# An attention output projection cut into seven half-size products in place of eight, with weight sums made by accumulating transfers

## The chip, the cores and the metric

The kernel runs on one core of a Trainium2 chip. The metric is device time in microseconds (us); lower is better. The engines are named as in the profile: PE (TensorE matmul), PEld (its weight load), DVE (VectorE), ACT (ScalarE), POOL (GpSimd), SP (SyncE, which only issues DMAs here).

## The reference

A decoder trunk of two layers on x of 512 tokens by 1024, in float32. Each layer is a token mixer and a SwiGLU FFN (1024 to 2816), each followed by a scaled residual and a layer norm:

```python
for i in range(2):
    if i == 0:
        h = multiscale_pool(x, pool_w, pool_scale)
    else:
        h = diff_attention(x, w_qkv, w_o, lam_p, subln_g, rel_table, lambda_init)
    x = layernorm(ALPHA * x + h)
    x = layernorm(ALPHA * x + (silu(x @ w_gate) * (x @ w_up)) @ w_down)
```

The causal differential attention has 8 heads with 128 value columns. Per head and token it forms `o`, divides by its root mean square, scales by `subln_g`, and puts the heads side by side to a 512x1024 matrix. Its last line is the matrix product that is changed, 512x1024 by 1024x1024:

```python
o = o * rsqrt(mean(o * o, axis=-1) + EPS)
o = o * subln_g * (1.0 - lambda_init)
return o.transpose(...).reshape(1, 512, 1024) @ w_o
```

## The kernel before

Every float32 operand is split into a high and a low part of a faster type: ACT casts x to the high part, and another engine subtracts to get the low part (`split`, lines 154 and 155). Every product is three matmuls into one PSUM bank: high by high, high by low, low by high (`mm3`, lines 180 to 182). The gate, up, down and value projections already use a seven-product scheme: both matrices are cut into two by two blocks, seven products of sums of blocks (named P1, P2, Q3, Q4, Q5, P6, P7) take the place of eight, and the sums are made beside the matmuls. The output projection does not: it multiplies whole.

All weights come from one tensor in DRAM, `wall`, as rows of 128x1024 in the order of `rows_of_wall`. `fetch` has SP load the next rows into a pool of 5 buffers (`raw`), `ready(upto)` splits them in that order into one of 6 pairs (`w96h`, `w96l`, ...). Of the rows listed in `by_dma` the low part is made by ACT (minus the raw value) and an accumulating DMA from GpSimd's queue (line 166), which adds the raw value from DRAM. All else keeps the order in which the code records it, on each engine. In the projection the rows are w96 to w103, one of each head; behind it come w104 and on, of the second FFN.

Attention goes head by head, with the work of neighbouring heads interleaved: `combine` and `split_values` prepare probabilities and values, `mix(h)` does the P·V products and the square of `o`, `root(h)` the sum of squares on PE and ACT's logarithm and exponential (lines 1372 and 1373, tile `rso`), `scaled(h)` the scaling on DVE and the split. Behind the last head's scores comes the projection. `gather(part, s, ws)` adds, for one block of 128 tokens and both column halves, the four heads of one part into two banks `wo`; part 0 is heads 0 to 3, part 1 heads 4 to 7. Between the products of part 0 stand what is left of heads 6 and 7. `residual` (line 214) adds a bank to the residual `res` on DVE, `stat`, `spread_of` and `norm` do the layer norm (POOL raises the variance to -1/2, line 230), and `turn` has PE transpose a block of the result (`pt`, line 267) for the FFN. The second FFN is called with `{0: 2, 2: 3}`: ahead of its first product it turns block 2, ahead of its third block 3.

Of the kernel before, what the change touches and what calls it, by code (L numbers as in the profile page):

```python
# [12 lines left out]
F32 = mybir.dt.float32  # L13
# [3 lines left out]
ALU = mybir.AluOpType  # L17

P = 128
# [49 lines left out]
AFFINE = {("P6", 2): (0, 1), ("P6", 3): (1, 1), ("Q3", 1): (2, 0), ("Q3", 2): (3, 0)}  # L69
GATE = ("P1", "Q5", "P6", "Q3", "P7", "P2", "Q4")  # L70
BEGUN = ("P6", "Q5", "P7", "Q3", "Q4")
PAIRS = [(0, 2), (2, 2), (4, 2), (6, 2), (8, 2), (10, 1)]


@with_exitstack
def trunk(ctx, tc, x, wall, pscale, lam_p, subln, table, lng, lnb, band, first, onehot, out):
# [6 lines left out]
    def bank(name):  # L83
        return ps.tile([P, 512], F32, tag="bank", name=name)
# [26 lines left out]
    raws = {}  # L111
    fetched = [0]
    divided = [0]
    attn = 2 + 3 * FB
    vrow = {c: attn + 2 * c for c in range(4)}
    qrow = attn + 8
# [12 lines left out]
    )  # L129
    rows_of_wall = [0, 1] + rows_of_ffn(0, 2)  # L130
    attn = len(rows_of_wall)
    rows_of_wall += order_of_rows + list(range(qrow + 2 * HEADS, qrow + 3 * HEADS))
    rows_of_wall += rows_of_ffn(1, qrow + 3 * HEADS)
    total = len(rows_of_wall)
    added = {attn + 6 + r: vrow[1] + r for r in range(2)}
    by_dma = {attn + c for c in (9, *range(12, 24))}

    def fetch(upto):
        while fetched[0] < min(upto, total):
            c = fetched[0]  # L140
            raws[c] = keep.tile([P, 1024], F32, tag="raw", name=f"raw{c}", bufs=RAWS)
            nc.sync.dma_start(out=raws[c], in_=wall[rows_of_wall[c]])
            if c in added:
                nc.gpsimd.dma_start(out=raws[c], in_=wall[added[c]], accum_op=ALU.add)
            fetched[0] += 1

    def split(dst_h, dst_l, src, scale=1.0, low=None):
        if scale != 1.0:
            nc.scalar.mul(dst_h, src, scale)
            nc.vector.scalar_tensor_tensor(  # L150
                dst_l, src, scale, dst_h.bitcast(F32), op0=ALU.mult, op1=ALU.subtract
            )
        else:
            nc.scalar.copy(dst_h, src)  # L154
            (low or nc.vector).tensor_tensor(dst_l, src, dst_h.bitcast(F32), op=ALU.subtract)  # L155

    def ready(upto, low=None):
        while divided[0] < min(upto, total):
            c = divided[0]
            fetch(c + RAWS)  # L160
            h, l = weight_pair(f"w{c}")
            raw = raws.pop(c)
            if c in by_dma:
                nc.scalar.copy(h, raw)
                nc.scalar.mul(l, raw, -1.0)
                nc.gpsimd.dma_start(
                    out=l, in_=wall[rows_of_wall[c]].bitcast(F32R), accum_op=ALU.add
                )
# [9 lines left out]
    def mm3(acc, a, b, start, stop):  # L178
        (ah, al), (bh, bl) = a, b
        nc.tensor.matmul(acc, ah, bh, start=start, stop=False)  # L180
        nc.tensor.matmul(acc, ah, bl, start=False, stop=False)  # L181
        nc.tensor.matmul(acc, al, bh, start=False, stop=stop)  # L182
# [138 lines left out]
    def turn(n, s, kept=None):  # L321
        transposed(n, s)
        turned(n, s, kept)
# [824 lines left out]
    def attention():  # L1148
        n = 2
        with tc.tile_pool(name="attn", bufs=1) as ap:  # L1150
# [52 lines left out]
            rest = xt[:, 1].rearrange("p i k t -> p (i k t)").rearrange("p (h i t) -> p h i t", h=4, i=2)  # L1203
            slots.update({16 + h: rest[:, h - 6] for h in (6, 7)})

            where = [base[0]]

# [158 lines left out]
            def root(h):  # L1366
# [6 lines left out]
                nc.scalar.activation(rs, rs, AF.Exp, scale=-0.5)  # L1373
                outs[h] = (acc, rs)

            def scaled(h):
                acc, rs = outs[h]
                nc.vector.scalar_tensor_tensor(rs, acc, gcol, rs, op0=ALU.mult, op1=ALU.mult)
                oh, ol = (slots[h if h < 6 else 16 + h][:, i, :] for i in range(2))
                split(oh, ol, rs)  # L1380
                outs[h] = (oh, ol)

            def gather(part, s, ws, between=lambda: None):
                acc = [bank(f"wo{part}_{s}_{d}") for d in range(2)]
                for js in ((0,), (1,), (2,), (3,)) if (part, s) == (0, 3) else (range(3), (3,)):
                    if js[-1] == (2 if (part, s) == (0, 3) else 3):
                        between()
                    for d in range(2):
                        for j in js:
                            mm3(  # L1390
                                acc[d],
                                tuple(t[:, s * P : (s + 1) * P] for t in outs[4 * part + j]),
                                tuple(t[:, d * 512 : (d + 1) * 512] for t in ws[j]),
                                j == 0,
                                j == 3,
                            )
                return acc

            def whole_x(t, a, b):
                nc.vector.tensor_tensor(  # L1400
# [87 lines left out]
            for h in range(HEADS):  # L1488
                if h > 0:
                    combine(h - 1, 3)  # L1490
                if h > 0:
                    split_values(h - 1)
                if h == 0:
                    scalars()
                if 1 < h <= SB + 1:
                    affine(n - 1, h - 2)
                if h == SB + 2:
                    load_gb(n)
                if h + 1 < HEADS:
                    load_bias(h + 1)  # L1500
                if h > 0:
                    accs = [bank(f"{nm}{h}") for nm in "qk"]
                    w = take(2)
                    ready(where[0] + {1: 3, last: 3}.get(h, 1))
# [5 lines left out]
                    ready(where[0] + {1: 4, last: 3}.get(h, 2))  # L1510
# [9 lines left out]
                    transposed(h - 1)  # L1520
                start_scores(h)
# [9 lines left out]
                if h == last:  # L1531
                    ready(where[0] + 4)
# [6 lines left out]
            cw = where[0]  # L1539
            combine(HEADS - 1, 3)  # L1540
            split_values(HEADS - 1)
            ws = take(4)
            between = [
                lambda: root(last - 1), lambda: transposed(last), lambda: mix(last),
                lambda: root(last),
            ]
            for s in range(SB):
                acc = gather(0, s, ws, between[s])
                if s == 0:
                    scaled(last - 1)  # L1550
                ready(cw + min(5 + s, WBUFS) if s < 3 else cw + 8)
                if s == 3:
                    scaled(last)
                for d in range(2):
                    residual(s, d, acc[d])
            ws = take(4)
            for s in range(SB):
                acc = gather(1, s, ws)
                if s == 0:
                    ready(where[0] + 1)  # L1560
                for d in range(2):
                    residual(s, d, acc[d], 1.0)
                    stat(n, s, d)
                spread_of(n, s)
                if 0 < s < 3:
                    turn(n, s - 1)
                norm(n, s)
                ready(where[0] + (min(s + 1, WBUFS - 4) if s < 3 else 4))
            base[0] = where[0]

    ffn(0, {3: 2, 5: 3})
    attention()
    ffn(1, {0: 2, 2: 3})


def buckets(rel):
# [27 lines left out]
def layout(w):  # L1604
# [37 lines left out]
    pieces.append(w["w_o"][0].reshape(HEADS, P, D))  # L1642
    ffn(1)
    return np.ascontiguousarray(np.concatenate(pieces, 0))

# [36 lines left out]
```

## Time and profile before

| | |
|---|---|
| time, median of 3 runs | 936.13 us (934.06 to 938.58) |
| profiled execution | 935.4 us, span 933.6 us |
| granted TensorE clock, mean | 0.998 |
| PE, PEld busy | 919.7, 821.5 us |
| DVE, ACT, POOL busy | 799.7, 521.0, 127.0 us |
| chain that ended last | PE 77%, DVE 12%, DMA 4%, ACT 3%, issue 2% |
| output projection | 540.5 to 590.4 us of the span |

Busy times are those of one profiled execution. A row of a timeline has start, length, engine, line, operation and tiles; a bracket behind it gives the idle time before it and what ended that. Matmuls overlap, so that the distance of two starts, not the length of one, is what a matmul takes of PE's time. A row of groups has the count, the sum, the mean of one in ns, and the idle time before.

### The profile page before, as it was taken

How to read it: one execution, taken by the hardware profiler on the slowest of the kernel's cores; microseconds unless marked ns; L12 is line 12 of the kernel's file. 1: busy time of each engine (PE TensorE's matmuls, PEld its weight loads, DVE VectorE, ACT ScalarE, POOL GpSimd, SP SyncE). 2: the span in 40 equal slices, each digit the busy share in tenths (PEclk: the TensorE clock that was granted, in tenths of full speed). 3: DMA queues.
4: the chain of work that ended last, by engine and by line, in shares of the span. 5: the costliest groups of instructions: out<-in, count | busy, mean ns of one | idle time of the engine just before them, and what ended most of it. 6: DMA issues, size and time to landing. Idle time of an engine off the chain costs nothing.

```text
span 933.6 us, 14893 instructions
## 1 busy us (share of the span) xinstructions
PE 919.7 (99%) x5662; PEld 821.5 (88%) x5662; DVE 799.7 (86%) x1186; ACT 521.0 (56%) x826; POOL 127.0 (14%) x152
## 2 busy tenths in 40 slices
PE   9999999999999999999999999999999999999996
PEld 8988899999988888888888888988999999988885
DVE  8999798999878978868888876889788999977888
ACT  6762445454564457667878854833445454654360
POOL 4221211110001201201111100212012110001101
PEclk9999999999999999999999999999999999999999
DMA  9497989986869988976666622587898996869952
GB/s 237 161 301 230 301 270 307 278 283 224 252 206 314 367 260 229 225 201 153 161 144 171 163 74 68 157 298 222 252 311 271 265 311 200 258 205 326 371 197 90
DMA packets 87765, 217.39 MB, mean 233 GB/s; under 512 B 15332, under 2 KB 26852, under 8 KB 87694
## 3 DMA queue, kind: packets, MB, share of 16 engines
q1 hardware_dynamic: 45148, 123.46, 39.3%
q0 software_dynamic: 18768, 58.20, 25.6%
q10 hardware_dynamic: 23778, 34.78, 10.4%
q8 instruction: 44, 0.72, 0.3%
q14 instruction: 27, 0.22, 0.1%
HBM read 179.70 MB, written 36.72 MB: 232 GB/s over the span
## 4 chain that ended last, share of the span: by engine, by line
PE 77%; DVE 12%; DMA 4%; ACT 3%; issue 2%; ACTq 0%; DVEq 0%; POOL 0%; SPq 0%
PE A L907 16%; PE P L1068 14%; PE C L907 7%; PE Q L1068 6%; PE B L907 4%; DMA raw<-in_wall 3%; DVE raw L697 2%; PE s L1293 2%; PE va L1224 2%; PE q L180 1%; PE q L182 1%; PE k L180 1%; PE k L182 1%; PE q L181 1%; PE k L181 1%
## 5 line engine op out<-in xcount | busy, mean ns | idle before, releaser
L697 DVE TENSOR_TENSOR raw<-raw,raw 128x1024 f32<-128x1024 f32 x64 | 78.2, 1222 | 10.3 <-DMA raw<-in_wall 9.4
L154 ACT CAST xs<-hid 128x512 fp32r<-128x512 f32 (+1 forms) x60 | 34.7, 581 | 24.6 <-DVE hid L874 24.6
L155 DVE TENSOR_TENSOR xs<-hid,xs 128x512 fp32r<-128x512 f32 (+1 forms) x60 | 38.4, 642 | 7.8 <-ACT xs L154 7.8
L1313 ACT ACTIVATE p<-p,mn 128x128 f32<-128x128 f32 (+3 forms) x64 | 35.2, 552 | 14.1 <-DVE mn L1308 14.1
L842 ACT CAST v<-u 128x512 fp32r<-128x512 f32 x22 | 13.7, 621 | 43.5 <-DVE u L840 43.5
L866 POOL DMA_DIRECT2D xs<-ssum x24 | 17.5, 727 | 141.8 <-PE Q L1068 120.0
L805 POOL DMA_DIRECT2D b<-in_wall x20 | 15.1, 810 | 147.8 <-DVE hid L1024 36.9
L805 POOL DMA_DIRECT2D hid<-in_wall x24 | 19.0, 832 | 103.5 <-DMA tsum<-hid 31.3
L230 POOL TENSOR_TENSOR rs<-rs,mhalf 128x1 f32<-128x1 f32 x16 | 12.8, 804 | 140.5 <-DVE rs L229 95.9
L1308 DVE CUSTOM_DVE_ANT_0 p<-s,bias 128x128 f32<-128x128 f32 (+3 forms) x64 | 28.1, 485 | 1.1 <-PE s L1293 1.1
L281 ACT ACTIVATE y<-pt,bT,gT 128x128 f32<-128x128 f32 x40 | 15.1, 456 | 15.8 <-PE pt L267 15.8
L221 DVE BATCH_NORM_STATS2 st<-res 128x6 f32<-128x512 f32 x32 | 22.2, 694 | 1.1
L1015 ACT COPY hid<-C 128x512 f32<-128x512 f32 x16 | 9.4, 588 | 22.9 <-PE C L907 17.1
L1029 ACT ACTIVATE sg<-A 128x512 f32<-128x512 f32 x16 | 9.6, 598 | 21.7 <-PE A L907 21.7
L757 ACT CAST xs<-hid 128x1024 fp32r<-128x1024 f32 x8 | 8.4, 1051 | 22.0 <-DVE hid L775 10.5
L806 POOL DMA_DIRECT2D b<-in_wall x10 | 12.3, 1230 | 56.3 <-DMA b<-in_wall 51.3
L806 POOL DMA_DIRECT2D hid<-in_wall x12 | 14.9, 1240 | 30.5 <-DMA hid<-in_wall 30.5
L1022 DVE TENSOR_TENSOR hid<-C,hid 128x512 f32<-128x512 f32 x16 | 11.0, 689 | 9.3 <-PE C L907 6.8
L1327 DVE SCALAR_TENSOR_TENSOR p<-p,sm,p 128x128 f32<-128x128 f32 (+3 forms) x32 | 17.7, 552 | 1.1
L155 POOL TENSOR_TENSOR sql<-sq,sqh 128x512 fp32r<-128x512 f32 x7 | 9.3, 1327 | 60.5 <-ACT sqh L154 60.5
L260 DVE TENSOR_TENSOR res<-res,gb 128x512 f32<-128x512 f32 (+1 forms) x20 | 16.0, 799 | 0.7
L844 DVE TENSOR_TENSOR v<-u,v 128x512 fp32r<-128x512 f32 x22 | 15.1, 686 | 1.4 <-ACT v L842 1.4
(1209 smaller groups left out, 3583.5 us busy)
## 6 DMA issues: line engine op xcount, KB each, us to landing
raw<-in_wall SPq DMA_DIRECT2D x130, 512.0 KB, 5.6
r<-tsum SPq DMA_DIRECT2D x40, 512.0 KB, 4.4
hid<-in_wall POOLq DMA_DIRECT2D x36, 512.0 KB, 6.9
b<-in_wall POOLq DMA_DIRECT2D x30, 512.0 KB, 6.7
r<-in_wall SPq DMA_DIRECT2D x30, 512.0 KB, 5.8
tsum<-hid ACTq DMA_DIRECT2D x24, 512.0 KB, 5.8
ssum<-v ACTq DMA_DIRECT2D x22, 512.0 KB, 4.9
tsum<-b ACTq DMA_DIRECT2D x20, 512.0 KB, 4.8
```

The source lines that it names most:

```text
L154: nc.scalar.copy(dst_h, src)
L155: (low or nc.vector).tensor_tensor(dst_l, src, dst_h.bitcast(F32), op=ALU.subtract)
L180: nc.tensor.matmul(acc, ah, bh, start=start, stop=False)
L181: nc.tensor.matmul(acc, ah, bl, start=False, stop=False)
L221: nc.vector.bn_stats(stats[n, s][:, d, :], res[:, s, d * 512 : (d + 1) * 512])
L697: tt(t, raws[pair[0]], raws[pair[1]], op=ALU.add)
L805: nc.gpsimd.dma_start(out=t[:, j], in_=src[:, j])
L806: nc.gpsimd.dma_start(out=t[:, 0], in_=src[:, :, 1], accum_op=ALU.add)
L907: nc.tensor.matmul(acc[:, f * 256 : (f + 1) * 256], w[:, c], x[:, kk, :], start=start and i == 0, stop=stop and i == len(todo) - 1, skip_g ...
L1068: nc.tensor.matmul(accs[s], x[:, k, r], y[:, c], start=first and k == 0 and e == 0, stop=last and k == m - 1 and e == 2, skip_group_check= ...
L1308: nc.vector.tensor_tensor_reduce(out=p, in0=accs[c], in1=biases[h][:, w - 1 :: -1] if w < S else biases[h][:, ::-1], op0=ALU.add, op1=ALU. ...
L1313: nc.scalar.activation(p, p, AF.Exp, bias=mn[:, q, c : c + 1], scale=-1.0, accum_out=sm[:, q, c : c + 1],)
```

## The change

The projection takes the seven-product scheme. The rows of the left matrix are token blocks 0, 1 and 2, 3; its columns heads 0 to 3 and 4 to 7; the right matrix is cut into 512x512 blocks W11, W12, W21, W22, and DRAM holds it so: a row pair per block, each row two heads by 512 columns. A product is 2 token blocks by 4 heads by 3 matmuls of 128x512, 24 in all (`product`, line 1533, banks `woc`, `wod`, `woe`): 168 in place of 192.

On the right side P1 uses W11, P2 W21 (rows w96 and w99), Q3 W22 (w100 and w101); Q5 uses W11+W12, P7 W12+W22, P6 W11+W12+W22, and Q4 the sum of all four. Accumulating DMAs from GpSimd's queue make these sums in float32: in a tile `wsum` of 128x2x1024, which is loaded once for P1 and Q5 and loaded again for P7 (`sum_step`), and in two of the five `raw` buffers that are kept aside, first for P6, then Q4 (`begin_apart`, `finish_apart`). Then they are split as before. `wsum` shares its buffer with the layer norm's gain and bias, whose load moves behind P7's split.

On the left side `scaled` and `sums_of` make the sums of a head's two halves on DVE and ACT, head by head in the attention loop; `split_sum` splits them. `read` adds each bank to its one or two places in `res` with the sign that it needs. The low parts of Q3's rows and of one FFN row move to GpSimd, and the last three rows with a low part by DMA are w96, w99 and w102. The second FFN turns blocks 2 and 3 ahead of its third and fourth product.

```diff
+BY_DMA = (0, 3, 6)
...
+    rows_of_wall += [mixw + r for r in (4, 2, 3, 5, 6, 7)]
...
+    by_dma |= {last_rows + c for c in BY_DMA}
...
-            fetch(c + RAWS)
+            fetch(c + RAWS - apart_rows[0])
...
+                if h < 4:
+                    nc.scalar.copy(comps[:, 0, h], first)
+                    nc.scalar.copy(sum_at("Q5", h, h + 1)[:, 0], halves(second))
+                    tt(sum_at("P7", h, h + 1)[:, 0], halves(first), halves(second), op=ALU.subtract)
+                    tt(comps[:, 1, h], first, comps[:, 0, h].bitcast(F32), op=ALU.subtract)
+                    return
+                if h < last - 1:
+                    sums_of(h)
+                    late_split(h)
...
+                tt(s1, s1, second, op=ALU.subtract)
+                nc.vector.scalar_tensor_tensor(
+                    s2, s3, -1.0, second, op0=ALU.mult, op1=ALU.subtract
+                )
+                if j > 1:
+                    tt(s4, first, s2, op=ALU.add)
...
+            def sum_step(step):
+                if not wsum:
+                    wsum.append(keep.tile([P, 2, D], F32, tag="gb", name="wsum"))
+                if step in (0, 2):
+                    r = mixw + step
+                    queue = nc.gpsimd if step else nc.sync
+                    queue.dma_start(
+                        out=wsum[0], in_=wall[r : r + 2].rearrange("r p t -> p r t")
+                    )
+                    return
+                r = mixw + (2 if step == 1 else 6)
+                for i in range(2):
+                    nc.gpsimd.dma_start(out=wsum[0][:, i], in_=wall[r + i], accum_op=ALU.add)
...
+            def product(p, js, accs, ts=(0, 1), by_term=False):
+                todo = [(e, t, j) for t in ts for j in js for e in range(3)]
+                if by_term:
+                    todo.sort(key=lambda x: x[0])
+                for e, t, j in todo:
+                    w = wparts[p, j // 2][e == 1]
+                    nc.tensor.matmul(
+                        accs[t], left_of(p, j, e // 2, t), w[:, j % 2 * 512 : j % 2 * 512 + 512],
...
+            mix(last)
+            split_sum("Q5", 2, 3)
+            split_sum("P6", 2, 3)
+            late_split(last - 1)
+            split_sum("P7", 0, 4)
+            product("P6", (0, 1), c)
+            row_weights("Q3", 0, nc.gpsimd)
+            sum_step(3)
+            finish_apart()
+            row_weights("Q3", 1, nc.gpsimd)
+            early_sums()
+            root(last)
+            product("Q5", (2,), d)
+            product("P6", (2,), c)
+            product("P2", (2,), e)
+            scaled(last)
+            sums_of(last)
+            split_sum("Q5", 3, 4)
+            split_sum("P6", 3, 4)
+            late_split(last)
+            split_sum("Q3", 0, 2)
+            product("Q5", (3,), d, by_term=True)
+            product("P6", (3,), c, by_term=True)
+            product("P2", (3,), e, by_term=True)
...
+            for i in range(2):
+                sum_weights("P7", i)
+            load_gb(n)
+            for t in range(2):
+                product("Q3", range(4), d, (t,))
...
+            apart_weights("Q4", 0)
+            ready(where[0] + 1)
...
+            for t in range(2):
+                product("P7", range(4), c, (t,))
+                read(2 + t, 1, c[t], op=ALU.subtract)
+            apart_weights("Q4", 1)
+            ready(where[0] + 2, nc.gpsimd)
+            norm(n, 1)
+            turn(n, 0)
...
+                product("Q4", range(4), c, (t,))
...
-    ffn(1, {0: 2, 2: 3})
+    ffn(1, {2: 2, 3: 3})
```

On ACT, before, behind the last head's P·V products (`sq` is the square of its output, `rso` its logarithm and exponential):

```order
L154 CAST w101h<-raw_5508 128x1024
L1362 ACTIVATE sq_5821<-o_5808 128x512
L154 CAST sqh_5822<-sq_5821 128x512
L1372 ACTIVATE rso_5852<-ss_5849,eps_t 128x512
L1373 ACTIVATE rso_5852<-rso_5852 128x512
L154 CAST w102h<-raw_5514 128x1024
L154 CAST w103h<-raw_5646 128x1024
L154 CAST xt<-rso_5852 128x512
```

At the same place in the changed kernel (casts of `vals` to `xt` are sums of heads to their high part, that of `rso_5721` is head 6):

```order
L1383 ACTIVATE sq_5826<-o_5813 128x512
L160 CAST sqh_5827<-sq_5826 128x512
L160 CAST xt<-vals 128x256 x2
L160 CAST heads<-rso_5721 128x512
L160 CAST xt<-vals 128x1024
L160 CAST w100h<-raw_5521 128x1024
L160 CAST w101h<-raw_5784 128x1024
L1393 ACTIVATE rso_5873<-ss_5870,eps_t 128x512
L1394 ACTIVATE rso_5873<-rso_5873 128x512
L160 CAST xt<-vals 128x256 x2
```

Six casts, two of them of weights, now stand between the square's cast and the logarithm of the last head.

On POOL, before, from head 6 to the second FFN (`sql` is the low part of a head's square, `rs` the power of the layer norm):

```order
L155 TENSOR_TENSOR sql_5475<-sq_5473,sqh_5474 128x512
L155 TENSOR_TENSOR sql_5667<-sq_5665,sqh_5666 128x512
L230 TENSOR_TENSOR rs_0_5923<-rs_0_5923,mhalf 128x1
L230 TENSOR_TENSOR rs_1_5960<-rs_1_5960,mhalf 128x1
L230 TENSOR_TENSOR rs_2_6027<-rs_2_6027,mhalf 128x1
L230 TENSOR_TENSOR rs_3_6088<-rs_3_6088,mhalf 128x1
```

And in the changed kernel from head 6 on (`raw_5202` and `raw_5325` are the two buffers kept aside):

```order
L161 TENSOR_TENSOR sql_5675<-sq_5673,sqh_5674 128x512
L172 DMA w99l<-in_wall 128x1024
L1474 DMA wsum<-in_wall 128x2x1024
L161 TENSOR_TENSOR w100l<-raw_5521,w100h 128x1024
L1480 DMA wsum<-in_wall 128x1024 x2
L1515 DMA raw_5202<-in_wall 128x1024
L1515 DMA raw_5325<-in_wall 128x1024
L161 TENSOR_TENSOR w101l<-raw_5784,w101h 128x1024
L236 TENSOR_TENSOR rs_0_5975<-rs_0_5975,mhalf 128x1
L172 DMA w102l<-in_wall 128x1024
L236 TENSOR_TENSOR rs_1_5996<-rs_1_5996,mhalf 128x1
L161 TENSOR_TENSOR w103l<-raw_5862,w103h 128x1024
```

Three low parts of weights and six transfers have come into this queue, ahead of and between the powers.

More of the change, by code (lines that the diff above doesn't have):

```diff
@@ L1374, in root, with two @@
                 outs[h] = (acc, rs)
+            def two(t):
+                return t.rearrange("p (a t) -> p a t", a=2)
             def scaled(h):
                 acc, rs = outs[h]
+                tt = nc.vector.tensor_tensor
                 nc.vector.scalar_tensor_tensor(rs, acc, gcol, rs, op0=ALU.mult, op1=ALU.mult)
[L1379 to L1397, printed above, removed]
@@ new lines, in finish_apart, with row_weights @@
+            def finish_apart():
+                for i in range(2):
+                    nc.gpsimd.dma_start(out=apart[i], in_=wall[mixw + 4 + i], accum_op=ALU.add)
+            def row_weights(p, i, low=None):
+                c = where[0]
+                ready(c + 1, low)
+                wparts[p, i] = parts[c]
+                where[0] += 1
+                if c == last_rows:
+                    apart_rows[0] = 2
+                    divided[0] += 2
+                    where[0] += 2
+            def product(p, js, accs, ts=(0, 1), by_term=False):
[6 more added lines that the diff above has]
+                        accs[t], left_of(p, j, e // 2, t), w[:, j % 2 * 512 : j % 2 * 512 + 512],
+                        start=p in ("P1", "Q5", "P2") and (j, e) == (0, 0),
+                        stop=p in ("Q4", "Q3", "P2") and (j, e) == (3, 2),
+                        skip_group_check=True,
+                    )
@@ L1538, in attention @@
                 combine(h, 2)
[L1539 to L1568, printed above, removed]
+            c = [bank(f"woc{t}") for t in range(2)]
@@ new lines, in attention @@
+            for t in range(2):
+                read(t, 0, c[t], ALPHA)
+            sum_weights("Q5", 1)
+            row_weights("P2", 1)
+            sum_step(2)
+            sums_of(last - 1)
+            apart_weights("P6", 1)
+            d = [bank(f"wod{t}") for t in range(2)]
+            product("Q5", (0, 1), d)
+            mix(last)
[4 more added lines that the diff above has]
+            product("P6", (0, 1), c)
@@ L1569, in attention @@
+            turn(n, 0)
+            for t in range(2):
+                stat(n, 2 + t, 1)
+            for t in range(2):
+                product("Q4", range(4), c, (t,))
+                if t == 0:
+                    turn(n, 1)
+                read(2 + t, 0, c[t], ALPHA)
+                stat(n, 2 + t, 0)
+                spread_of(n, 2 + t)
+                norm(n, 2 + t)
+                ready(where[0] + 3 + t)
             base[0] = where[0]
```

143 lines of the change are left out of this document (133 added, 10 removed).

## The prediction

> **What bounds the kernel now.** I read the page's first and fourth parts, then the windows cut at the stage that is changed.
>
> ```profile
> span 933.6 us, 14893 instructions
> PE 919.7 (99%) x5662; PEld 821.5 (88%) x5662; DVE 799.7 (86%) x1186; ACT 521.0 (56%) x826; POOL 127.0 (14%) x152
> PE 77%; DVE 12%; DMA 4%; ACT 3%; issue 2%; ACTq 0%; DVEq 0%; POOL 0%; SPq 0%
> 540.50:590.40 49.90, 49.81 (x235) 40.89 (x234) 37.99 (x67) 27.02 (x51) 3.66 (x4) 1.00 0.23 74
> 590.40:603.70 13.30, 13.30 (x113) 13.30 (x113) 10.65 (x16) 11.83 (x26) 4.82 (x6) 1.00 0.57 176
> ```
>
> The last two rows are the output projection and the start of the FFN behind it; their columns are length, then PE, PEld, DVE, ACT and POOL busy, granted clock, DMA share, GB/s. PE works 49.81 of 49.90 us at clock 1.00, the others have slack. A PE that never waits gets shorter by whatever matmul time is taken away, as long as no wait opens. The table of PE's waits over the whole program:
>
> ```profile
> PE A L907 <- DVE hid L1024: 3.1, 3, 1.4
> PE pt L267 <- DVE res L239: 0.2, 1, 0.2
> ```
>
> The second is the only one in this stage; PE's timeline shows it at 577.5:
>
> ```profile
> 540.46 0.40 PE L180 MATMUL wo<-w96h,heads 128*128 128x512 f32 x1
> 559.04 0.40 PE L180 MATMUL wo<-w99h,heads 128*128 128x512 f32 x1
> 567.05 0.39 PE L180 MATMUL wo<-w101h,heads 128*128 128x512 f32 x1
> 577.03 0.39 PE L182 MATMUL wo<-w103h,xt 128*128 128x512 f32 x1
> 577.50 0.77 PE L267 MATMUL pt<-ident,res 128*128 128x128 f32 x5
> ```
>
> From 567.05 to 577.03 lie 44 matmuls, so one takes 9.98/44 = 0.2268 us, and the gap before 577.50 is 577.50-577.03-0.23 = 0.24.
>
> **The part that goes.** Eight half-size products are 192 matmuls, seven are 168. 24 x 0.2268 = 5.44 us go, and with the 0.24 wait (the transposes now stand behind 24 matmuls more) 5.68. What follows are the waits that may open. Times are in before's frame; the stage starts at 540.46, and I keep PE's order of after.
>
> **Term 1, the last head.** Ahead of the last head's P·V products 48 projection matmuls stand instead of 66, so these end 18 x 0.2268 = 4.1 earlier, at 554.95 for 559.04. Its output still goes through ACT, DVE and ACT before PE can use it:
>
> ```profile
> 559.30 0.60 ACT L1362 ACTIVATE sq<-o 128x512 f32<-128x512 f32 x1 [5.82 <-PE o L182]
> 559.93 0.62 ACT L154 CAST sqh<-sq 128x512 fp32r<-128x512 f32 x1
> 563.82 0.69 ACT L1372 ACTIVATE rso<-ss,eps_t 128x512 f32<-128x512 f32 x1 [3.27 <-PE ss L1370]
> 564.54 0.63 ACT L1373 ACTIVATE rso<-rso 128x512 f32<-128x512 f32 x1
> 565.08 1.03 ACT L154 CAST w102h<-raw 128x1024 fp32r<-128x1024 f32 x1
> 566.02 1.04 ACT L154 CAST w103h<-raw 128x1024 fp32r<-128x1024 f32 x1
> 566.15 1.23 DVE L155 TENSOR_TENSOR w102l<-raw,w102h 128x1024 fp32r<-128x1024 f32 x1 [3.60 <-ACT w102h L154]
> 568.42 0.75 DVE L1378 SCALAR_TENSOR_TENSOR rso<-o,gcol,rso 128x512 f32<-128x512 f32 x1
> L155 DVE TENSOR_TENSOR al<-at,ah 128x256 fp32r<-128x256 f32 x8 | 3.3, 415 | 0.0
> L154 ACT CAST ah<-at 128x256 fp32r<-128x256 f32 x8 | 3.2, 401 | 0.0
> ```
>
> Before, ACT idled 3.27 us between the square's cast and the logarithm. In after six casts stand there: two of 256 columns, one of 512, one of 1024 and the two weight casts w100h and w101h. By start distances of these rows: square 0.63, its cast 0.53, 256-wide ones 0.6, 512-wide 0.51, 1024-wide 0.95, weights 2 x 0.95, logarithm 0.72, exponential 0.66: from 555.2 to 561.7. DVE's scaling (0.77) and first sum (0.45) and ACT's cast of it (0.43) end at 563.35. PE meanwhile has 32 matmuls, until 554.95 + 7.26 = 562.2. It waits **1.15**: 1.9 of the chain are the weight casts. I keep 0.6 to 1.6, as the narrow casts may cost 0.3 or 0.45 each.
>
> **Term 2, weights of Q3 on GpSimd.** Two low parts of 128x1024 move to GpSimd's queue, with four accumulating transfers between them. Their prices:
>
> ```profile
> L155 POOL TENSOR_TENSOR sql<-sq,sqh 128x512 fp32r<-128x512 f32 x7 | 9.3, 1327 | 60.5 <-ACT sqh L154 60.5
> L155 POOL TENSOR_TENSOR w2l<-raw,w2h 128x1024 fp32r<-128x1024 f32 x1 | 3.5, 3455 | 0.6 <-ACT w2h L154 0.6
> 446.41 0.86 POOL L166 DMA_DIRECT2D w86l<-in_wall  x1 [3.96 <-ACT w86l L165]
> 450.03 0.85 POOL L166 DMA_DIRECT2D w87l<-in_wall  x1 [2.75 <-ACT w87l L165]
> 513.69 0.86 POOL L166 DMA_DIRECT2D w94l<-in_wall  x1 [3.92 <-ACT w94l L165]
> 517.31 0.85 POOL L166 DMA_DIRECT2D w95l<-in_wall  x1 [2.75 <-ACT w95l L165]
> w86l<-in_wall POOLq DMA_DIRECT2D x1, 512.0 KB, 6.8
> w87l<-in_wall POOLq DMA_DIRECT2D x1, 512.0 KB, 5.7
> w94l<-in_wall POOLq DMA_DIRECT2D x1, 512.0 KB, 6.9
> w95l<-in_wall POOLq DMA_DIRECT2D x1, 512.0 KB, 7.7
> tall<-in_wall POOLq DMA_DIRECT2D x3, 1024.0 KB, 12.5
> tall<-in_wall SPq DMA_DIRECT2D x1, 1024.0 KB, 7.3
> ```
>
> A low part takes 2 x 1.33 = 2.66 to 3.46; I take 3.0, since seven of the eight instances run at the shorter rate. ACT's w100h ends at 559.45, GpSimd's low part at 562.45, the four issues (4 x 0.86) at 565.9, the second low part at 568.9. Q3 starts at 563.35 + 18 x 0.2268 = 567.43 and reads that part at its eighth matmul, 569.0. Ahead of the first accumulate GpSimd also needs the reload of the weight sum, 1 MB issued at 554.9: at SP's 7.3 it is there at 562.2, at the 12.5 of GpSimd's own queue at 567.4, and everything behind it moves by 5, which I leave to the slower rival below. Behind the second low part GpSimd has block 0's power, asked for only once Q3's first half is read (some 572), so nothing there is late. I take **0.3** (0 to 1.9: the 3.46 for both low parts and a reload 1 us later).
>
> **Terms 3 and 4, the weight sums of P7 and Q4.** The first accumulate, issued at 562.45 and 6.3 under way (the mean of 6.8 and 5.7), lands at 568.8; with 1.05 for ACT and 1.2 for DVE the first row of P7 is ready at 571.1. PE reaches P7 at 567.43 + 5.44 + 0.3 = 573.2, its second row at 574.8, where that row may be up to 0.3 late: **0**. The others follow at the spacing of two transfers. The rows above give landings at 453.2 and 455.7, and at 520.6 and 525.0: 2.5 and 4.4 apart, from issues 3.6 apart; nothing in before issues four at once. With a spacing s the fourth lands at 568.8 + 3s, and Q4's second row is ready 2.25 later; PE reads it after P7 (5.44), one turn (0.82) and six matmuls more, at 581.2. At s = 3 it is ready at 580.1, hidden by 1.1, but DVE takes the low parts in turn with PSUM reads, statistics and a normalization (0.8 each). I take **0.6**, from 0 (s = 2.5) to 3.6 (s = 4.4). The Trainium skill, "DMA: Bandwidth & Descriptors", section Anatomy of one DMA, puts a GpSimd-issued transfer at 2.0 us plus bytes/436e3, an estimate of 3.2 for 512 KB; by it this term would be 0 and the time 932.3, but the rows of this trace have 5.7 to 7.7 and decide.
>
> **Term 5, the hand-over.** Block 3's normalization waits for GpSimd's power, then DVE, then PE's turn, as before:
>
> ```profile
> 593.20 0.15 DVE L229 TENSOR_SCALAR rs<-mv 128x1 f32<-128x1 f32 x1
> 594.09 0.81 DVE L239 TENSOR_SCALAR res<-res,mv,rs 128x1024 f32<-128x1024 f32 x1 [0.73 <-POOL rs L230]
> ```
>
> The second FFN now takes turns 2 and 3 one product pair or more later, which covers most of this. I take **0.4** (0 to 1.2: the wait for the power and a cast). The rest of the diff (sums for heads 0 to 6 on DVE and ACT, some 1.2 us a head by the 128x256 rows) lies in stages where PE does not wait and DVE has slack; nothing is charged for it, and 0.5 if that cover is gone.
>
> Sum: -5.44 - 0.24 + 1.15 + 0.3 + 0 + 0.6 + 0.4 = **-3.2**. The profiled execution took 935.4 (span 933.6 and 1.8 around it), so 932.2; from the median 936.13, **932.9**.
>
> **The rivals.**
> *All waits hidden:* the weight casts fit behind the logarithm's wait and the transfers come close together. For it: ACT's 3.27 us hole, and the 2.5 spacing. Against: the row order puts the two weight casts ahead of the logarithm. 936.13 - 5.68 = 930.4. Chance 0.2.
> *The sums of Q4 land late:* spacing 4.4, which the second pair of rows shows with SP's loads beside it. Term 4 is 3.6 instead of 0.6: 935.9. Chance 0.13.
> *Slower:* accumulating transfers go at the rate of the 1 MB row, 12.5 us or 6.2 per 512 KB. The fourth lands at 568.8 + 18.6 = 587.4, Q4's second row is ready at 589.6 against 581.2: 8.4 of wait instead of 0.6, so about 940.8. It eats the whole gain from a spacing of 4.65 on, and is slower by over 0.5% from 6.2, or if the reload takes 12.5 as well. Against it: w86l to w95l are accumulating transfers and took 5.7 to 7.7. Chance 0.1. The Trainium skill, "TensorE: Matmul & The Clock Gate", Part 1, has the array fall to half clock after some 3.4 us of idling and stay there about as long; by that such a wait would cost an estimated 1.7 us more. The row at the head has clock 1.00, with no wait here over 0.24, so no run yet shows it.
> *The second FFN gives it back:* loads start no earlier there, and PE already waits 3.1 for DVE; its chain of waits has loads in it:
>
> ```profile
> 695.76 4.63 DMA raw<-in_wall
> 704.14 9.42 DMA raw<-in_wall
> ```
>
> If arrival of weights sets that stage, the gain of 3.2 is used up: 936.1. Against it: PE's waits there name no load. Chance 0.07.
> That the change doesn't do what it says is excluded: PE's order has 168 matmuls.
>
> **How the numbers follow.** The forecast keeps 0.5. A measurement of this kernel can tell about 0.5% from no change, 4.7 us: faster is below 931.45, slower above 940.81. Faster: the hidden rival (0.2) and 0.06 of the forecast whose terms come out near their lower ends. Slower: the third rival from a spacing of 6.2, with a late reload, 0.1. The rest is 0.64. The range goes from 929.8 (930.4, less 0.6 as a part of the 3.1 that PE waits for `hid`, whose order against the moved turns changes) to 937.5: terms 1 and 2 at upper ends (+0.45, +1.6) with term 4 at s = 4 (+2.5).
>
> **What would show it.** Right: PE waits of about 1.2 at the first matmul of Q5's fourth head, on ACT; below 1 at Q3's second row, on GpSimd; up to 1 at Q4's second row; 168 matmuls at 0.227. Wrong: accumulates that land over 4.4 apart; a wait at the first row of P7; PE waits in heads 5 to 7, where I charge none; a second FFN longer than before.

## The result, and the profile after

The changed kernel takes 942.49 us (median of 4, 940.58 to 943.67) against 935.1 for the one before (median of 4, one run more than above): a ratio of 1.0075, 95% interval 1.0053 to 1.0098. The forecast was 932.9, with 937.5 as its upper end. The page of the profiled execution:

```profile
span 939.9 us, 14927 instructions
PE 918.7 (98%) x5638; PEld 819.4 (87%) x5638; DVE 815.9 (87%) x1209; ACT 534.2 (57%) x848; POOL 147.7 (16%) x169
PE 65%; DVE 17%; DMA 7%; issue 6%; ACT 3%; POOL 1%; ACTq 1%; DVEq 0%; POOLq 0%; SPq 0%
```

24 matmuls are gone from PE, and the chain that ended last now runs through DVE for 17% where it was 12%. PE's four longest waits (total, times, longest; one of 1.9 at the start of both kernels is left out):

```profile
PE wod L1533 <- DVE xt L161: 3.6, 1, 3.6
PE wod L1533 <- ACT xt L160: 2.6, 1, 2.6
PE A L913 <- DVE hid L1030: 2.5, 4, 1.1
PE woc L1533 <- DVE oQ41l L161: 1.6, 1, 1.6
```

Three are new, 7.72 us together, all in the projection. PE's timeline has them here, with what follows the second:

```profile
566.10 0.73 PE L1533 MATMUL wod<-oQ51h,xt 128*128 128x512 f32 x2 [2.56 <-ACT xt L160]
570.89 1.22 PE L1533 MATMUL wod<-oQ51h,xt 128*128 128x512 f32 x2 [3.60 <-DVE xt L161]
571.91 1.05 PE L1533 MATMUL woc<-oP61h,xt 128*128 128x512 f32 x2
575.29 0.62 PE L1533 MATMUL woe<-w99h,heads 128*128 128x512 f32 x2
575.75 0.39 PE L1533 MATMUL wod<-w100h,xt 128*128 128x512 f32 x1
590.83 0.50 PE L1533 MATMUL woc<-oQ41l,heads 128*128 128x512 f32 x1 [1.56 <-DVE oQ41l L161]
```

From 570.89 to 575.75 stand 14 matmuls in 4.86 us, 3.18 at the usual 0.2268: 1.7 are lost to the clock. The stage by windows of the two kernels, from the first projection matmul to the first of the second FFN, and the 9 us around that wait (length, PE, PEld, DVE, ACT, POOL, clock, DMA share, GB/s); the first row is the kernel before, the others the changed one:

```profile
540.46:591.25 50.79, 50.70 (x244) 41.78 (x243) 38.80 (x68) 27.55 (x52) 3.66 (x4) 1.00 0.23 73
```
```profile
541.47:595.72 54.25, 46.53 (x212) 37.61 (x211) 51.77 (x78) 36.51 (x64) 17.52 (x13) 0.94 0.77 194
566.00:575.00 9.00, 5.31 (x15) 3.98 (x16) 8.89 (x10) 3.84 (x7) 4.54 (x4) 0.62 1.01 203
```

PE went from always busy to waiting, DVE from 38.8 of 50.8 us to 51.8 of 54.3, POOL from 3.7 to 17.5. Why DVE is so busy stands in its timeline. The changed kernel's POOL subtractions:

```profile
560.68 3.26 POOL L161 TENSOR_TENSOR w100l<-raw,w100h 128x1024 fp32r<-128x1024 f32 x1 [3.87 <-ACT w100h L160]
566.90 3.64 POOL L161 TENSOR_TENSOR w101l<-raw,w101h 128x1024 fp32r<-128x1024 f32 x1
587.29 2.40 POOL L161 TENSOR_TENSOR w103l<-raw,w103h 128x1024 fp32r<-128x1024 f32 x1
```

and what DVE did at the same times:

```profile
560.96 0.68 DVE L1444 TENSOR_TENSOR vals<-heads 128x512 f32<-128x512 f32 x1
561.67 2.81 DVE L1445 TENSOR_TENSOR vals<-vals 128x512 f32<-128x512 f32 x1
566.32 4.85 DVE L161 TENSOR_TENSOR xt<-vals,xt 128x256 fp32r<-128x256 f32 x2
587.76 3.01 DVE L161 TENSOR_TENSOR oQ41l<-raw,oQ41h 128x1024 fp32r<-128x1024 f32 x1
```

L1445 is as large as L1444, which took 0.68; the 128x256 pair takes 0.75 elsewhere, oQ41l's size 1.22. Each of the three meets a subtraction on POOL and ends 0.5 to 1.1 us behind POOL's end, about its own length. (Of the pair the first subtraction alone takes 4.52 and ends 0.30 behind.) The lost time is 2.1 + 4.1 + 1.8 = 8.0 us of DVE, and each of PE's three waits stands behind one of them, the first of the three only in part, as e1 will show.

Executions differ by some us in where the projection starts (539.8 to 545.4; 539.8 to 541.9 in before and in e2, e8 and e12, which change nothing ahead of it); so kernels are also compared by a stage length, from the first projection matmul to the first matmul on g_5 in the second FFN (541.47 to 615.19 in the changed kernel). Each ratio is to runs of the kernel before on the same chip, whose median went from 934.56 to 935.29, so that ratios compare experiments better than medians do:

| kernel | median us | ratio to before (95%) | stage us |
|---|---|---|---|
| before | 935.1 | | 68.7 |
| changed | 942.49 | 1.0075 (1.0053, 1.0098) | 73.7 |
| e1 lows on DVE | 936.27 | 1.0016 (0.9998, 1.0034) | 68.7 |
| e2 before, lows on POOL | 935.50 | 1.0007 (0.9995, 1.0020) | 69.4 |
| e3 FFN's low on DVE | 939.04 | 1.0057 (1.0030, 1.0084) | 72.3 |
| e4 casts late | 937.61 | 1.0030 (1.0015, 1.0046) | 70.3 |
| e5 order for DVE | 935.97 | 1.0013 (0.9993, 1.0033) | 69.3 |
| e6 reload by SP | 936.49 | 1.0013 (0.9990, 1.0036) | 68.4 |
| e7 lows ahead | 940.99 | 1.0072 (1.0047, 1.0098) | 72.5 |
| e8 24 fewer, late | 935.28 | 1.0009 (0.9994, 1.0023) | 68.7 |
| e9 FFN's low by DMA | 935.72 | 1.0009 (0.9996, 1.0022) | 67.8 |
| e10 three lows left out | 933.07 | 0.9982 (0.9970, 0.9994) | 66.1 |
| e11 two lows by DMA | 934.91 | 0.9999 (0.9986, 1.0013) | 67.9 |
| e12 24 fewer, early | 931.19 | 0.9956 (0.9937, 0.9976) | 65.3 |

### The profile page after: what moved, and what is told of

Same layout as the page of the kernel before. It is cut to its first block, busy times and chain, and to the rows that moved or that the text cites. A ratio compares the mean times of both kernels' runs of the same rounds, so it can differ in the third digit from the quotient of the medians.

```text
span 939.9 us, 14927 instructions
## 1 busy us (share of the span) xinstructions
PE 918.7 (98%) x5638; PEld 819.4 (87%) x5638; DVE 815.9 (87%) x1209; ACT 534.2 (57%) x848; POOL 147.7 (16%) x169
## 3 DMA queue, kind: packets, MB, share of 16 engines
q10 hardware_dynamic: 23778, 34.78, 10.2%
## 4 chain that ended last, share of the span: by engine, by line
PE 65%; DVE 17%; DMA 7%; issue 6%; ACT 3%; POOL 1%; ACTq 1%; DVEq 0%; POOLq 0%; SPq 0%
PE A L913 14%; PE P L1074 14%; PE Q L1074 6%; PE C L913 6%; DMA raw<-in_wall 5%; PE B L913 3%; DVE raw L703 3%; PE va L1245 2%; PE s L1314 2%; PE q L186 2%; PE q L188 2%; PE k L186 2%; PE k L188 2%; PE q L187 2%; PE k L187 2%
## 5 line engine op out<-in xcount | busy, mean ns | idle before, releaser
L287 ACT ACTIVATE y<-pt,bT,gT 128x128 f32<-128x128 f32 x40 | 15.0, 456 | 13.2 <-PE pt L273 11.9
L763 ACT CAST xs<-hid 128x1024 fp32r<-128x1024 f32 x8 | 8.4, 1051 | 21.7 <-DVE hid L781 10.2
```

## The experiments

Theory A: a subtraction of two SBUF tiles on POOL and one on DVE exclude each other, and behind that DVE's work, not PE's, sets the length of the projection. Theory B: the accumulating transfers stretch DVE's rows, or their arrival makes PE wait.

**e1, the three low parts back on DVE.**

```diff
-            row_weights("Q3", 0, nc.gpsimd)
+            row_weights("Q3", 0)
...
-            row_weights("Q3", 1, nc.gpsimd)
+            row_weights("Q3", 1)
...
-            ready(where[0] + 2, nc.gpsimd)
+            ready(where[0] + 2)
```

> The three low parts w100l, w101l and w103l go from POOL to DVE, at the same places of the code; the casts, the accumulating transfers and everything else stay. Theory A (a subtraction of two SBUF tiles on POOL and one on DVE exclude each other): DVE's stretched rows return to their usual lengths (L1445 2.81 to 0.7, the 128x256 pair 4.85 to 0.75, oQ41l 3.01 to 1.2), PE's wait of 3.60 for the low part falls under 0.5, the 1.56 in Q4 falls under 0.5, the slow clock shrinks with them; the 2.56 stays, since two 1.2 us subtractions now stand ahead of the early sums on DVE. About 936. Theory B (the accumulating transfers, six of them issued by POOL, hold DVE): the rows stay stretched where transfers are issued, and DVE has 3.6 us more to do: 942 or more.

DVE's timeline, the rows that were stretched, and POOL's transfers beside them:

```profile
564.16 0.69 DVE L1445 TENSOR_TENSOR vals<-vals 128x512 f32<-128x512 f32 x1
566.69 0.75 DVE L161 TENSOR_TENSOR xt<-vals,xt 128x256 fp32r<-128x256 f32 x2
584.10 1.22 DVE L161 TENSOR_TENSOR oQ41l<-raw,oQ41h 128x1024 fp32r<-128x1024 f32 x1
564.30 1.76 POOL L1480 DMA_DIRECT2D wsum<-in_wall  x2 [7.27 <-DMA wsum<-in_wall]
565.43 2.39 POOL L1515 DMA_DIRECT2D raw<-in_wall  x2
```

All three are back at their lengths, with the same four accumulates issued beside the first and the second: B's first half falls, as far as transfers alone go. 6.2 us of the 7.4 are gone (5.5 by the ratios). PE keeps one wait in the projection over 0.5, 2.70 for ACT's cast of the last head, with the slow clock behind it (eight matmuls in 3.34 us, 1.81 at full speed). The time is as expected, within 0.3 us; the slow clock, which was to shrink with the waits, stayed (1.5 lost for 1.7).

**e2, the same on the kernel before.**

```diff
-                ready(cw + min(5 + s, WBUFS) if s < 3 else cw + 8)
+                ready(cw + min(5 + s, WBUFS) if s < 3 else cw + 8, None if s < 3 else nc.gpsimd)
```

> The kernel before with one edit: the low parts w102l and w103l, made on DVE at 566.15 and 567.29, are made on POOL; no transfer is issued by POOL there. Theory A: POOL takes about 2.4 us for each, and DVE's next subtraction of two SBUF tiles (xt<-rso,xt, 0.69 before) is stretched to over 2 us, while DVE instructions with a PSUM input keep their lengths; PE, which never waited here, waits 2 to 4 us; about 938. Theory B: no transfer, so xt<-rso,xt keeps 0.69; PE waits under 1.5 for the longer subtraction on POOL alone.

POOL, then DVE:

```profile
565.55 2.43 POOL L155 TENSOR_TENSOR w102l<-raw,w102h 128x1024 fp32r<-128x1024 f32 x1 [22.48 <-ACT w102h L154]
567.92 2.90 POOL L155 TENSOR_TENSOR w103l<-raw,w103h 128x1024 fp32r<-128x1024 f32 x1
566.97 1.55 DVE L155 TENSOR_TENSOR xt<-rso,xt 128x512 fp32r<-128x512 f32 x1 [1.66 <-ACT xt L154]
568.45 1.27 DVE L214 SCALAR_TENSOR_TENSOR res<-res,wo 128x512 f32<-128x512 f32 x2
569.64 2.26 DVE L155 TENSOR_TENSOR w104l<-raw,w104h 128x1024 fp32r<-128x1024 f32 x1
```

No transfer is near, and the effect is there, in both directions: `xt<-rso,xt` (0.69 before) ends at 568.52, about its length behind POOL's first; POOL's second takes 2.90 for 2.43, since it waits for that; w104l (1.22) takes 2.26 and ends 1.1 behind POOL's second. The two PSUM reads between them (L214, one SBUF tile, one PSUM bank) run beside POOL at their usual 0.64 each. The stretch of `xt<-rso,xt` was smaller than expected (1.55, not over 2), because DVE came to it 1.0 before POOL's end, and PE waited only 0.55, for w102l itself, not 2 to 4. The time is that of before (1.0007), not 938. The mechanism is shown, its price is a matter of when the two meet.

**e3, only the third subtraction back on DVE**, the last line of e1's edit.

> Only w103l, the low part of the FFN's second row, goes from POOL to DVE. Theory A: oQ41l goes from 3.01 to 1.2 us and the wait of 1.56 in Q4 falls under 0.5, the two waits ahead of Q3 stay at 2.6 and 3.6: about 941. Theory B: unchanged at 942.5, since oQ41l has an accumulating transfer near it all the same.

oQ41l is at 1.2 us and its wait gone, L1445 still at 2.81. The median fell by 3.5 us, the ratio by 1.7 us and the stage by 1.4, where 1.5 was expected. That the sum fits is luck in part: in place of oQ41l's wait another of 1.20 opened at Q4's first matmul, for ACT's `y` of a turn, and the two waits ahead of Q3, which were to stay, came out smaller: 2.19 for the first and, for the second, two of 0.19 and 1.16, since the instruction that met w101l was now a later one (the last head's low part, 4.76).

**e4, as e1, with the weights of Q3 behind the last head's chain.**

```diff
-            row_weights("Q3", 0)
             sum_step(3)
             finish_apart()
-            row_weights("Q3", 1)
-            early_sums()
             root(last)
...
             late_split(last)
+            row_weights("Q3", 0)
+            early_sums()
...
             split_sum("Q3", 2, 4)
+            row_weights("Q3", 1)
```

> As e1, and the split of w100 and w101 (casts on ACT, low parts on DVE) and the early sums move behind the last head's logarithm, scaling and sums. If ACT's two weight casts and DVE's early sums are what is left of the first wait, it falls from 2.6 to under 0.8, and what comes next is the accumulating transfers: P7's rows, landing some 8 and 11 us after the reload, are then late by 1 to 2 us. About 933.5. By theory B 941 or more.

The first wait is gone altogether, so the two weight casts and the early sums made it. But a new one of 3.28 stands at Q3's first matmul, for DVE's reads of bank `wod`: the work put behind the last head now stands ahead of these. Missed: 937.6, not 933.5. Moving DVE's work moves the wait.

**e5, an order for DVE**: w100's cast ahead of the logarithm, w101's behind it, both low parts on DVE behind the last head's sums (w101's behind the reads of `wod`), the split of P7's left side behind the reads of `woc`, and P7's weight sums split beside the reads of `woe`, one each.

```diff
-            split_sum("P7", 0, 4)
             product("P6", (0, 1), c)
-            row_weights("Q3", 0, nc.gpsimd)
+            row_cast("Q3", 0)
             sum_step(3)
             finish_apart()
-            row_weights("Q3", 1, nc.gpsimd)
             early_sums()
             root(last)
...
             late_split(last)
+            row_low("Q3", 0)
+            row_cast("Q3", 1)
...
                 read(2 + t, 1, d[t], ALPHA)
+            row_low("Q3", 1)
...
                 read(t, 1, c[t], ALPHA, ALU.subtract)
+            split_sum("P7", 0, 4)
...
-            for i in range(2):
-                sum_weights("P7", i)
+                sum_weights("P7", t)
...
-            ready(where[0] + 2, nc.gpsimd)
+            ready(where[0] + 2)
```

> The changed kernel with no weight subtraction on POOL and another order on DVE and ACT: w100's cast before, w101's behind the last head's logarithm, both low parts on DVE behind the last head's sums, the split of P7's left side and the reads of bank woe moved behind Q3's start. Theory A (POOL's subtractions shut DVE out, and without them DVE, not PE, bounds the stretch from the last head to Q3): the work that need not be there is out of the way, PE's first wait falls from 2.7 under 0.5 and Q3's under 0.5; the accumulating transfers are then next, with 0.5 to 2 us at P7's second row. 932 to 933.5. Theory B (some other step bounds this stretch): a wait of 2 us or more stays ahead of Q3, 935 to 937.

The waits ahead of Q3 and the slow clock are gone, as A has it; four waits of 0.4 to 1.35 at P7 and Q4, 3.2 together, take their place, all but one for DVE. 935.97, not 932 to 933.5: A's first half holds, but of what came next only the 0.6 for ACT's cast of P7's second row can be a transfer's.

**e6, the reload of wsum by SP, in two transfers.**

```diff
-                    queue = nc.gpsimd if step else nc.sync
-                    queue.dma_start(
-                        out=wsum[0], in_=wall[r : r + 2].rearrange("r p t -> p r t")
-                    )
+                    for i in range(2):
+                        nc.sync.dma_start(out=wsum[0][:, i], in_=wall[r + i])
```

> As e5, and the reload of wsum is issued by SP, as two transfers of 512 KB, in place of one of 1 MB by POOL. If the reload (8.3 us from issue to landing) holds up the four accumulating transfers, these begin 2 to 4 us earlier and the wait at P7's second row goes: 0.5 to 1.5 faster than e5. If the DMA engines are full anyway, no change against e5.

The sums land earlier (ACT casts P7's second row at 568.75), and the time is no better than e5's (0.9 in the stage length, nothing in the median). The longer waits of e6's projection, and its window:

```profile
PE woc L1544 <- DVE res L1553: 1.4, 1, 1.4
PE woc L1544 <- DVE oP71l L161: 0.8, 1, 0.8
PE woc L1544 <- DVE oP70l L161: 0.4, 1, 0.4
540.04:589.03 48.99, 45.81 (x213) 36.19 (x211) 47.09 (x81) 36.31 (x64) 8.72 (x9) 1.00 0.86 213
```

oP71h is there at 569.8, and oP71l is made at 573.94, in its turn: DVE works 47.1 of 49.0 us. The transfers are not what PE waits for.

**e7, w101's low part ahead of the four accumulates on POOL.**

```diff
             row_weights("Q3", 0, nc.gpsimd)
+            row_weights("Q3", 1, nc.gpsimd)
             sum_step(3)
             finish_apart()
-            row_weights("Q3", 1, nc.gpsimd)
```

> The changed kernel with one edit: w101's low part stands ahead of the four accumulating transfers on POOL, no longer behind them; both are still on POOL. If the issues make POOL's subtraction longer (3.64 in place of about 2.4) and so DVE's wait, DVE's stretched instruction takes about 2.5 to 3 in place of 4.85 and PE's 3.60 wait falls under 1.5, but P7 and Q4 get their sums some 1 to 3 us later: 939 to 941. If the issues have no part in it, POOL still takes 3.6 for w101l and the time is 941 to 943.

```profile
564.32 2.84 POOL L161 TENSOR_TENSOR w101l<-raw,w101h 128x1024 fp32r<-128x1024 f32 x1
564.82 0.74 DVE L1403 SCALAR_TENSOR_TENSOR rso<-o,gcol,rso 128x512 f32<-128x512 f32 x1
565.59 1.85 DVE L1428 TENSOR_TENSOR vals<-vals,rso 128x256 f32<-128x256 f32 x1
```

Without issues ahead of it POOL takes 2.84, and DVE's second stretch falls from 4.1 to 1.4 us (1.85 for 0.42). L1403, with PSUM's `o`, runs through. The first wait grows instead, to 3.7, since the stretched row now stands in the last head's chain, and the 14 matmuls behind it take 6.08 us for 3.18; 940.99, at the upper end of what was expected.

**e8 and e12, the kernel before without 24 of its matmuls**: the third term of three heads is left out, of the second half of the projection in e8, of the first in e12.

```diff
-                            mm3(
...
+                            nc.tensor.matmul(acc[d], ah, bh, start=j == 0, stop=False)
+                            nc.tensor.matmul(acc[d], ah, bl, start=False, stop=False)
+                            if part == 0 or j == 3:
+                                nc.tensor.matmul(acc[d], al, bh, start=False, stop=j == 3)
```

(e12 has `part == 1` there.)

> The kernel before without 24 of its 192 projection matmuls: the third term (low by high) of heads 4, 5 and 6 is left out. It adds nothing else. If removed matmuls are worth their 0.2268 us each and the second FFN takes the gain over, 24 x 0.2268 = 5.4 faster than before, about 929. If the second FFN gives the gain back, 932 or more.

> The kernel before without 24 matmuls, as e8, but of the first half of the projection: the third term of heads 0, 1 and 2 is left out. If in e8 the layer norm's chain (reads, statistics, power, normalization) behind the second half took the gain, 24 x 0.2268 = 5.4 is won here but for the last head's chain on ACT and DVE, which is exposed by 1 to 3: 931 to 933. If DVE's work as a whole bounds this stretch in before as well, no gain: 934 to 935.

e8 wins nothing. PE's waits in its projection:

```profile
PE pt L267 <- DVE res L239: 4.2, 4, 1.6
PE wo L1394 <- ACT xt L154: 0.6, 1, 0.6
```

Where the second half's blocks get shorter, each turn waits for its block's reads, statistics and normalization on DVE. e12, with as many left out earlier, wins 4.1 of the 5.4 (935.29 to 931.19 on the same chip), so the second FFN does not give it back, and a matmul is worth its price where DVE's chain has room:

```profile
PE wo L1394 <- DVE res L214: 0.9, 1, 0.9
PE pt L267 <- DVE res L239: 0.4, 2, 0.3
541.15:588.53 47.38, 46.09 (x220) 36.96 (x219) 38.81 (x68) 27.47 (x52) 3.66 (x4) 1.00 0.25 78
```

**e9 to e11, less work for DVE, from e6.** e9 makes w103's low part by ACT and an accumulating transfer (`BY_DMA = (0, 3, 6, 7)`), e11 w100's as well; e10 leaves out three subtractions and has PE read another row's low part in their place.

> As e6, and the low part of the FFN's second row (w103) is made by ACT and an accumulating transfer, not by DVE: 1.13 us of DVE's work less, just ahead of block 1's normalization. Theory A (DVE's queue of work bounds the projection): the wait for the turn falls by 0.4 and the time by 0.4 to 1.0 against e6. Theory B (PE's waits in e6 are latencies of transfers): no change.

> As e6, with three subtractions of 128x1024 left out on DVE (the low parts of w101, of P7's second row and of Q4's second row; PE reads the first row's low part in their place, so the matmuls stay): 3.4 us of DVE's work less. Theory A: PE's waits at P7 and Q4 (together 3.4 in e6) fall under 1 and the time falls by 2 to 3 us against e6, under that of before: about 932. Theory B: the waits stay, since the sums' transfers land no earlier: less than 0.7 faster than e6.

> As e9, and w100's low part is also made by ACT and an accumulating transfer. DVE has 2.3 us less to do than in e6. Theory A: 1 to 2 us faster than e6, 932.5 to 934, unless the transfer, issued at 559 and 7 us under way, is late at Q3's second matmul (566.3) by up to 1. Theory B: no faster than e6.

e10, 3.4 us of DVE's work less, is 3.4 us faster than e6 (2.9 by the ratios to before) and under the kernel before, 933.07 for the expected 932; the waits at P7 are gone, one of 1.3 for a read in Q4 stays:

```profile
PE woc L1552 <- DVE res L1561: 1.3, 1, 1.3
```

e9 and e11 are 0.8 and 1.6 faster than e6 (0.4 and 1.3 by the ratios, within their intervals), the way that A has it, though e11's 934.91 is above the 932.5 to 934 expected. In e11 w100's transfer is 0.6 late at Q3. e11 computes all of the reference and equals the kernel before (0.9999); none that does was faster.

## Why the prediction was wrong, by its own steps

**The step that failed** is the one on what POOL costs: "A low part takes 2 x 1.33 = 2.66 to 3.46". I priced the moved subtractions for POOL's queue and asked only when their results are needed, not what DVE does meanwhile. The 3.46 was no price at all. Before's own trace has it:

```profile
16.41 3.46 POOL L155 TENSOR_TENSOR w2l<-raw,w2h 128x1024 fp32r<-128x1024 f32 x1 [0.60 <-ACT w2h L154]
16.35 1.22 DVE L155 TENSOR_TENSOR pw1l<-raw,pw1h 128x1024 fp32r<-128x1024 f32 x1
```

DVE starts a subtraction of two SBUF tiles 0.06 earlier and ends at 17.57; POOL's row lasts to 19.87, 2.3 behind that, and 2.4 is what it takes undisturbed (587.29 above). It was a wait, and the row that I quoted as the upper end of a duration was the sign of the exclusion. Three of POOL's shorter rows (508.44, 525.24, 542.41) run beside DVE rows with a PSUM input. The Trainium skill, "SBUF — State Buffer", section Who interferes with whom, states that a DVE instruction with two SBUF inputs contends with a GpSimd instruction that reads SBUF, and, in section SBUF: two separate sides, that whichever of the two starts first gets the ports for the whole instruction and the other blocks. The rows of the changed kernel, e2 and e7 agree that the two shut each other out; it was the rule that spoke against this change, and I did not weigh it. Who is first cannot be read from the starts of the rows: L1444 starts 0.28 behind POOL's w100l and keeps its 0.68, and POOL's end less 2.40 puts its work at 561.54, near L1444's end (561.64).

**The second step** is "the others have slack": no term of the sum charges DVE for its new work. DVE had 11.9 us less to do than PE in this stage of before, but the change adds work there: 38.8 us become 47.3 in e1, where nothing is stretched (541.68 to 590.92, 49.24 long), mostly weight splits and left-side sums. Without the matmuls PE is busy for 45.8 (e6), so DVE has more to do than PE. I took 5.44 us off PE and charged DVE nothing; its work was the bound to sum. The forecast was 3.2 us below before and the result is 7.0 above it by the ratio: taking POOL's subtractions away gives back 5.5 of these 10.2 (e1), and of the other 4.7 e10 gives back 2.9 (against e6), by taking 3.4 us of work off DVE.

The terms:
- Removal, 5.44: e12 shows 4.1 where DVE has room, e8 none where it has not. The matmuls went, at 0.227 each.
- Term 1, 1.15: measured 2.56. The scaling, which could start at 562.8 behind the exponential, started at 564.41, behind L1445; without that 1.6 the wait would be 0.9. With the row back at its length (e1) the wait is 2.70, as DVE does w100 and w101 itself there.
- Term 2, 0.3: no wait of PE's for w101l; in its place 3.60, through DVE.
- Terms 3 and 4: the reload landed at 564.4, not 562.2, and ACT's casts of the sums start at 571.35, 574.15 and 576.62, a spacing of 2.5 to 2.8, near the 3 that I took. The transfers were no wait of PE's in the changed kernel; the 1.56 in Q4 is the third stretched row, so that a wait at the place that I named there is luck. The result is near the 940.8 of the rival of slow accumulates by luck too: nothing of its mechanism happened. (The list of POOL's queue above has seven transfers, six accumulating ones and the reload.)
- Term 5, 0.4: from turn 2 or the FFN's first product to g_5, two turns included, 18.76 before and 19.47 after: 0.7.
- Not in the sum: the clock, 1.7. I had it only as an addition to the slow rival.
- Two slips in the sums change nothing here: by the terms as they stand Q4's second row is read at 580.8 (573.2 + 5.44 + 0.82 + 1.36), not 581.2, and the upper end of the range adds 2.5 for s = 4 to a sum that already holds 0.6 of it.

Stage: -5.44 - 0.24 + 7.72 + 1.7 + 0.7 = +4.4, against 5.0 measured; 0.6 is not accounted for. 1.0 of the span's 6.3 lies ahead of the stage, in the profiled execution's first 10 us (PE's row `pool<-bh` starts at 10.33 for 9.26), and 0.3 behind it. The rival of the second FFN fell: behind g_5 before takes 324.4 us and the changed kernel 324.7.

Open: in the changed kernel the first subtraction of DVE's pair starts at 566.32 and takes 4.52, while POOL's row starts only at 566.90, behind the four accumulates, and takes 3.64. e3 has the same with another row of DVE (the first row below is the changed kernel, the others e3):

```profile
565.80 2.37 POOL L1515 DMA_DIRECT2D raw<-in_wall  x2
564.84 2.37 POOL L1515 DMA_DIRECT2D raw<-in_wall  x2
565.94 3.68 POOL L161 TENSOR_TENSOR w101l<-raw,w101h 128x1024 fp32r<-128x1024 f32 x1
565.41 4.76 DVE L161 TENSOR_TENSOR heads<-rso,heads 128x512 fp32r<-128x512 f32 x1
```

POOL's end less its undisturbed 2.40 is 568.14 in the changed kernel and 567.22 in e3, and the issue of the last accumulates ends at 568.17 and 567.21. So DVE was held for 1.8 us in both while POOL was still issuing, although the issues alone held nothing in e1. e7 shows that their place matters (2.84 for POOL, and 1.4 of DVE's time for 4.1), not what holds DVE in these 1.8 us: of the 4.1 the transfers may have a part, with a subtraction queued behind them. It was not tried apart.

## What to carry to other kernels

Before work leaves a bounding engine, sum what every other engine will have to do in the same stretch, in the new order: PE at 99% with DVE at 76% left room for 11.9 us, and the change took 5.4 on one side and added 8.5 on the other (e1, with every subtraction on DVE). A helper engine is free only if its instructions and those of the engine that it helps do not shut each other out; look in the trace for rows of one operation that take two lengths, and at what the other engine does during the longer one. To know what a removed piece is worth, leave it out of the old kernel first: e8 and e12 cost one edit each, and gave 0 and 4.1 us for 24 matmuls each.

## What the runs showed of the hardware

- POOL's subtraction of two 128x1024 SBUF tiles takes 2.40 us undisturbed; a DVE instruction with two SBUF tiles as inputs that meets it ends about its own length behind POOL's end, whatever its size (0.42 became 1.85 in e7, 0.69 became 2.81 and 1.22 became 3.01 in the changed kernel), and POOL in turn waits for one that DVE has begun (2.90 for 2.43 in e2). DVE instructions with one SBUF tile and one PSUM bank are not affected (0.64 in e2, 0.74 in e7), nor is DVE by the issue of accumulating transfers alone (0.75 for the pair in e1).
- A wait of PE of 2.2 us (e3), 2.70 (e1) or 3.60 was followed by matmuls at about half speed for some 3 us, 1.5 to 1.7 us lost, and one of 3.67 (e7) by 6.1 us, 2.9 lost; waits of up to 1.6 (e8) were not, nor were the four matmuls between the 2.56 and the 3.60. The Trainium skill, "TensorE: Matmul & The Clock Gate", Part 1, gives an idle window of about 3.4 us; here less was enough.
